# Attention groups 1 and 2 of a hybrid trunk: scores by residue in blocks of 64 by 64, three transposes a half, both groups' values stacked

## The chip, the cores and the metric

The kernel runs on one core of one Trainium2 chip. Its time is the device time of one execution in microseconds (us); the median of the runs is quoted, and the trace is of one profiled execution. In the profile PE is the matrix engine TensorE (PEld its weight loads), DVE is VectorE, ACT ScalarE, POOL GpSimd, SP the engine that issues most DMAs.

## What is computed

Two residual layers on a sequence of 256 tokens of width 1024: a short gated convolution, then a dilated window attention, each followed by a squared-ReLU MLP of width 4096 and a gated per-layer embedding. The change lies in the attention alone. It has three groups of 8 heads of width 128; group g sees keys at distances that are multiples of its dilation, within its window:

```python
DILATED_PATTERNS = ((128, 1), (512, 4), (2048, 16))
...
for g, (window, dilation) in enumerate(DILATED_PATTERNS):
    o_g, lse_g = dilated_window_attention(q[:, :, g], k[:, :, g], v[:, :, g], window, dilation)
    outs.append(o_g)
    lses.append(lse_g)
weights = jax.nn.softmax(jnp.stack(lses, axis=0), axis=0)
o = jnp.sum(weights[..., None] * jnp.stack(outs, axis=0), axis=0)
return o.reshape(b_, s_, hh * dh).astype(h.dtype) @ w_o
```

Weighting the groups by the softmax of their log sums is the same as one softmax over the scores of all three groups side by side, and that is how the kernel does it. With dilation 4, a token meets only tokens of its own residue modulo 4, 64 of the 256; with dilation 16, a part of these.

## The kernel before

A plan, a list of matmul blocks and of steps (`do`), is written out by `make_plan` and walked once; each block names a weight tile, an accumulator and an operand. Weights come from HBM in slabs of up to 8 tiles of 128x128 on SP's queue, and each slab is split into two fp32r halves, `whi` on ScalarE (line 357) and `wlo` on VectorE (line 296), up to five slabs ahead of use. All projections are line 393, in `block`. PSUM is one pool of 8 banks, given out in turn.

In the attention layer the tokens lie in the order of `residue_order`: first by residue modulo 4, so that tokens of one residue are 64 neighbours, and a half of 128 tokens holds two residues. Head after head the plan runs the projections of q and k for groups 0, 1 and 2 (`acc_qk`) and of v (`acc_v`), and between them, one head behind, the steps `scores`, `turn` and `values` of the head before.

- `scores` (lines 674 to 693), for each half b of 128 queries: group 0 as three fp32r matmuls against all 256 keys (L680), then groups 1 and 2 each as one fp32 matmul of the half's 128 queries against the half's 128 keys (L683). The scores fill a bank of 512 columns: 256 of group 0, 128 of group 1, 128 of group 2. One VectorE instruction (L686) scales, adds the mask and takes the maximum; ScalarE takes the exponential with its sum (L690) and scales by the reciprocal (L692). The mask sets to -1e30 what a group does not see, so half of each 128x128 block of groups 1 and 2, where the residues differ, is masked.
- `turn` (lines 695 to 707) transposes the 128x512 probabilities of each half in four pieces (L701), splits those of group 0 in two, and copies those of groups 1 and 2 out of PSUM on ScalarE (L706).
- `values` (lines 709 to 734): group 0 as six fp32r matmuls (L716), then for each half and each of groups 1 and 2 one fp32 matmul (L722), all into one accumulator; ScalarE and VectorE split the result into `y` (L733, L734).
- `v_out` (lines 662 to 671) scales the v projection out of PSUM: group 0 in two halves (L668, L669), groups 1 and 2 as one ScalarE copy of 128x256 for each half of the tokens (L670).

A scheduler orders the instructions of each engine; PE's order follows the plan closely.

Of the kernel before, what the change touches and what calls it, by code (L numbers as in the profile page):

```python
# [9 lines left out]
F32 = mybir.dt.float32  # L10
F32R = mybir.dt.float32r
I32 = mybir.dt.int32
AF = mybir.ActivationFunctionType
ALU = mybir.AluOpType

P = 128
S = 256
# [5 lines left out]
GROUPS = 3  # L23
# [3 lines left out]
NEG = -1e30  # L27
# [13 lines left out]
def residue_order(t):  # L41

    return (t % 4) * 64 + (t % 16 // 4) * 16 + t // 16
# [211 lines left out]
def tile_trunk(ctx: ExitStack, tc: tile.TileContext, plan, slabs, ap, out):  # L255
    nc = tc.nc
# [3 lines left out]
    apool = ctx.enter_context(tc.tile_pool(name="act", bufs=ACT_BUFS))  # L260
# [6 lines left out]
    def act(name, dtype=F32):  # L267
        return apool.tile([P, 2, S], dtype, tag="act", name=name)
# [4 lines left out]
    def pair(name, tag="pair", dtype=F32R):  # L273

        if tag == "pair":
            t = apool.tile([P, 2, 2, S], dtype, tag=tag, bufs=PAIR_BUFS, name=name)
        else:
            t = cpool.tile([P, 2, 2, S], dtype, tag=tag, bufs=1, name=name)
        return t[:, :, 0, :], t[:, :, 1, :], t

    def bank(name):
        return psum.tile([P, 2, S], F32, tag="ps", name=name)
# [6 lines left out]
    def f32(t):  # L289
        return t.bitcast(F32)  # L290

    def flat(t):
        return t.rearrange("p i s -> p (i s)")
# [20 lines left out]
    rstd, rows, cur, mask, by_token = {}, {}, {}, {}, {}  # L314
# [5 lines left out]
    offsets, n = [], 0  # L320
# [6 lines left out]
    for si, s in enumerate(slabs):  # L327
# [3 lines left out]
        at = 0  # L331
# [71 lines left out]
    def close(name):  # L403
        opened.discard(name)

        return acc.pop(name)
# [21 lines left out]
    def split_into(kind, j, src):  # L428
        hi, lo, t = pair(f"{kind}{j}", "pp" if kind in ("p0", "p1") else "pair")
        nc.scalar.activation(hi, src, AF.Copy)  # L430
        sub(lo, src, hi)
        state[kind][j] = (hi, lo, t)
# [146 lines left out]

    def masks_load():  # L580
        for b in (0, 1):
            mask[b] = apool.tile([P, 512], F32, tag="act", name=f"mask{b}")
            nc.sync.dma_start(mask[b], ap["mask"][:, b, :])

    def conv(c):
# [75 lines left out]

    def v_out(head):

        v0, v12 = act(f"v0_{head}", F32R), act(f"v12_{head}")
        for b in (0, 1):
            p, r = flat(close(("v", b, head))), rstd[3][:, b : b + 1]
            hi, lo = v0[:, b, :P], v0[:, b, P:]
            nc.scalar.activation(hi, p[:, :P], AF.Copy, scale=r)  # L668
            nc.vector.scalar_tensor_tensor(lo, p[:, :P], r, f32(hi), ALU.mult, ALU.subtract)  # L669
            nc.scalar.activation(v12[:, b, :], p[:, P : GROUPS * P], AF.Copy, scale=r)  # L670
        cur["v", head] = v0, v12


    def scores(head):
        for b in (0, 1):
            own = slice(b * P, (b + 1) * P)
            ps = psum.tile([P, 512], F32, tag="ps", name=f"sc{head}_{b}")
            hi, lo, _ = state["qk"][head]
            for n, (q, k) in enumerate(((hi, hi), (hi, lo), (lo, hi))):
                nc.tensor.matmul(ps[:, :S], q[:, 0, own], k[:, 1, :], start=n == 0, stop=n == 2)  # L680
            for g in (1, 2):
                t = cur["qk", head, g]
                nc.tensor.matmul(ps[:, (g + 1) * P : (g + 2) * P], t[:, 0, own], t[:, 1, own], start=True, stop=True)  # L683
            sm = flat(act(f"sm{head}_{b}"))
            stats = [spool.tile([P, 1], F32, tag=f"st{n}_{b}", name=f"st{n}_{head}_{b}") for n in range(3)]
            nc.vector.tensor_tensor_reduce(  # L686
                out=sm, in0=ps, in1=mask[b], op0=ALU.add, op1=ALU.max, scale=SCALE, scalar=NEG, accum_out=stats[0]
            )
            nc.vector.tensor_scalar(stats[1], stats[0], -1.0, None, ALU.mult)
            nc.scalar.activation(sm, sm, AF.Exp, bias=stats[1], accum_out=stats[2])  # L690
            nc.vector.reciprocal(stats[2], stats[2])
            nc.scalar.activation(sm, sm, AF.Copy, scale=stats[2])  # L692
            cur["pr", head, b] = sm

    def turn(head):

        ps = [bank(f"tp{head}_{n}") for n in (0, 1)]
        for b in (0, 1):
            sm = cur.pop(("pr", head, b))
            for n in range(4):  # L700
                nc.tensor.transpose(  # L701
                    ps[n // 2][:, n % 2, b * P : (b + 1) * P], sm[:, n * P : (n + 1) * P], ident
                )
        split_into("pT", head, ps[0])
        t = act(f"pT12_{head}")
        nc.scalar.activation(t, ps[1], AF.Copy)  # L706
        cur["pT12", head] = t

    def values(head):
        ps = bank(f"o{head}")  # L710
        v0, v12 = cur.pop(("v", head))
        hi, lo, _ = state["pT"].pop(head)
        for kb in (0, 1):
            vhi, vlo = v0[:, kb, :P], v0[:, kb, P:]
            for n, (a, b) in enumerate(((vhi, hi), (vhi, lo), (vlo, hi))):
                nc.tensor.matmul(  # L716
                    ps[:, 0, :], a, b[:, kb, :], start=kb == 0 and n == 0, stop=False, skip_group_check=True
                )
        t = cur.pop(("pT12", head))
        for b in (0, 1):  # L720
            for g in (0, 1):
                nc.tensor.matmul(  # L722
                    ps[:, 0, b * P : (b + 1) * P],
                    v12[:, b, g * P : (g + 1) * P],
                    t[:, g, b * P : (b + 1) * P],
                    start=False,
                    stop=g == 1,
                    skip_group_check=True,
                )
        if head % 2 == 0:  # L730
            state["y"][head // 2] = pair(f"y{head // 2}")
        hi, lo = (t[:, head % 2, :] for t in state["y"][head // 2][:2])
        nc.scalar.activation(hi, ps[:, 0, :], AF.Copy)  # L733
        nc.vector.tensor_tensor(lo, ps[:, 0, :], f32(hi), ALU.subtract)  # L734
# [76 lines left out]
    def last_scale(b, c):  # L811
# [12 lines left out]
    steps = dict(  # L824
        begin=begin, p_in=p_in, x_in=x_in, add_up=add_up, squares=squares, proj_out=proj_out, stat=stat, stat_rows=stat_rows, conv=conv, mix_out=mix_out, up_out=up_out,
        down_out=down_out, gate_out=gate_out, rope=rope, masks=masks_load, qk_out=qk_out, qk_split=qk_split, v_out=v_out,
        scores=scores, turn=turn, spread=spread, values=values,
        last_load=last_load, turn_h=turn_h, last_gate=last_gate, last_out=last_out, last_rms=last_rms, last_scale=last_scale,
    )
# [21 lines left out]
def masks():  # L851

    import numpy as np

    t = np.argsort([residue_order(t) for t in range(S)])
    m = np.full((P, 2, 512), NEG, np.float32)
    for b in range(2):
        q = t[b * P : (b + 1) * P, None]
        for keys, to, window, step in (
            (t, slice(0, S), 128, 1),  # L860
            (t[b * P : (b + 1) * P], slice(S, S + P), 512, 4),
            (t[b * P : (b + 1) * P], slice(S + P, S + 2 * P), 2048, 16),
        ):
            d = q - keys[None]
            m[:, b, to][(d >= 0) & (d <= window) & (d % step == 0)] = 0.0
    return m


# [56 lines left out]
```

## Time and profile before

| | |
|---|---|
| runs, median | 780.3 us (780.16 to 780.39, 3 runs) |
| profiled execution, its own time | 780.49 us |
| its span, first to last instruction | 778.6 us |
| busy: PE / PEld | 770.2 us / 700.2 us |
| busy: DVE / ACT / POOL | 572.8 us / 442.7 us / 166.8 us |
| HBM read | 139.10 MB, 180 GB/s over the span |

Busy time is the sum in which an engine had an instruction under way. Matmul records overlap: the next one starts before the record of the last ends, so PE's busy time does not say what one matmul costs. The chain of waits does: it follows the work back from the last instruction and gives each piece the time until the next. "mean ns of one" in the groups is the length of a record, and "idle before" the idle time of the engine just before it.

### The profile page before, as it was taken

To read this page: it belongs to the slowest core of one execution; us is meant where nothing else is said; L and a number is where in the kernel's file an instruction comes from. 1 tells how busy PE (TensorE), PEld (TensorE's weight loads), DVE (VectorE), ACT (ScalarE), POOL (GpSimd) and SP (SyncE) were. 2 spreads that over 40 slices of the span, in tenths; PEclk is the share of its full clock that TensorE was granted. 3 is DMA by queue.
4 is the path that set the end of the run, shared out by engine and by line. 5 is a ranking of instruction groups with operands and counts; after the bars stand their busy time and mean duration, and the time that the engine had idled before them with its cause. 6 is when DMAs were issued, how large, how long until landed. Compare 5 with 4: busy or idle time off the path is not lost.

```text
span 778.6 us, 12434 instructions
## 1 busy us (share of the span) xinstructions
PE 770.2 (99%) x4812; PEld 700.2 (90%) x4812; DVE 572.8 (74%) x823; ACT 442.7 (57%) x685; POOL 166.8 (21%) x110
## 2 busy tenths in 40 slices
PE   9999999999999999999999999999999999999996
PEld 9998998888888899989989989989988888888885
DVE  6898779898556669788768768767698887655564
ACT  8655565565444447557655655655675555444453
POOL 0000000000000000177867867865000000000002
PEclk9999999999999999999999999999999999999999
DMA  9865555656555654654455455455465555555521
GB/s 315 301 193 187 189 190 186 192 175 205 184 191 185 192 179 152 204 186 154 149 175 163 151 174 163 153 172 191 134 200 184 189 189 191 188 190 189 188 92 54
DMA packets 42538, 140.95 MB, mean 181 GB/s; under 512 B 4848, under 2 KB 6128, under 8 KB 42480
## 3 DMA queue, kind: packets, MB, share of 16 engines
q1 hardware_dynamic: 41904, 139.52, 55.2%
q8 instruction: 37, 0.61, 0.3%
q10 hardware_dynamic: 576, 0.66, 0.3%
q14 instruction: 21, 0.17, 0.1%
HBM read 139.10 MB, written 1.05 MB: 180 GB/s over the span
## 4 chain that ended last, share of the span: by engine, by line
PE 98%; issue 1%; DVE 0%; POOL 0%; POOLq 0%; DVEq 0%
PE acc_u L393 23%; PE acc_d L393 23%; PE acc_qk L393 17%; PE acc_v L393 9%; PE acc_o L393 6%; PE acc_g L393 5%; PE acc_B L393 3%; PE acc_C L393 3%; PE acc_X L393 3%; PE acc_p L393 1%; PE o L722 1%; PE sc L683 1%; PE tp L701 1%; PE sc L680 1%; PE o L716 1%
## 5 line engine op out<-in xcount | busy, mean ns | idle before, releaser
L296 DVE TENSOR_TENSOR wlo<-raw,whi 128x1024 fp32r<-128x1024 f32 (+2 forms) x277 | 350.6, 1272 | 159.7 <-ACT whi L357 157.4
L357 ACT ACTIVATE whi<-raw 128x1024 fp32r<-128x1024 f32 (+2 forms) x277 | 278.5, 1007 | 214.7 <-PE acc_d L393 77.1
L393 PE MATMUL acc_u<-x,whi 128*128 128x512 f32 x512 | 160.8, 395 | 0.0
L393 PE MATMUL acc_d<-u,whi 128*128 128x512 f32 x512 | 160.8, 395 | 0.0
L393 PE MATMUL acc_qk<-x,whi 128*128 128x512 f32 (+1 forms) x432 | 134.5, 368 | 0.0
L393 PEld LDWEIGHTS acc_d<-u,wlo 128*128 128x128 f32 x512 | 96.2, 188 | 22.7
L393 PEld LDWEIGHTS acc_u<-x,wlo 128*128 128x128 f32 x512 | 96.2, 188 | 22.6
L463 POOL TENSOR_TENSOR n<-v,power 128x2 f32<-128x2 f32 (+1 forms) x6 | 3.9, 651 | 518.2 <-DVE v L488 513.5
L393 PE MATMUL acc_qk<-x,wlo 128*128 128x256 f32 x384 | 107.8, 281 | 0.0
L393 PE MATMUL acc_u<-x,wlo 128*128 128x256 f32 x512 | 101.3, 278 | 0.0
L393 PE MATMUL acc_d<-u,wlo 128*128 128x256 f32 x512 | 100.9, 278 | 0.0
L393 PEld LDWEIGHTS acc_qk<-x,whi 128*128 128x128 f32 x432 | 77.9, 188 | 13.7
L650 POOL TENSOR_TENSOR rot<-qk,sinr 16x512 f32<-16x512 f32 x44 | 78.3, 1781 | 3.0
L393 PEld LDWEIGHTS acc_u<-x,whi 128*128 128x128 f32 x512 | 78.0, 189 | 0.0
L393 PEld LDWEIGHTS acc_d<-u,whi 128*128 128x128 f32 x512 | 77.9, 189 | 0.0
L393 PEld LDWEIGHTS acc_qk<-x,wlo 128*128 128x128 f32 x384 | 72.5, 189 | 0.0
L393 PE MATMUL acc_v<-whi,x 128*128 128x384 f32 x256 | 68.9, 340 | 0.0
L647 POOL TENSOR_TENSOR qk<-qk,cosr 128x512 f32<-128x512 f32 x22 | 36.8, 1671 | 53.7 <-DVE qk L413 41.8
L393 PEld LDWEIGHTS acc_v<-whi,x 128*128 128x128 f32 x256 | 46.6, 188 | 0.0
L393 PE MATMUL acc_o<-y,whi 128*128 128x256 f32 x256 | 46.4, 283 | 0.0
L656 POOL TENSOR_TENSOR qk<-qk,rot 48x512 f32<-48x512 f32 x22 | 42.9, 1950 | 1.7
L393 PE MATMUL acc_v<-wlo,x 128*128 128x384 f32 x128 | 42.9, 335 | 0.0
(175 smaller groups left out, 1028.9 us busy)
## 6 DMA issues: line engine op xcount, KB each, us to landing
raw<-in_w SPq DMA_DIRECT2D x230, 512.0 KB, 3.4
raw<-in_w SPq DMA_DIRECT2D x32, 384.0 KB, 3.1
raw<-in_w SPq DMA_DIRECT2D x10, 256.0 KB, 5.1
h<-in_xT SPq DMA_DIRECT2D x4, 256.0 KB, 5.6
mask<-in_mask SPq DMA_DIRECT2D x2, 256.0 KB, 4.4
gain<-in_gain SPq DMA_DIRECT2D x2, 256.0 KB, 5.9
out<-htg SPq DMA_DIRECT2D x2, 256.0 KB, 2.1
raw<-in_w ACTq DMA_DIRECT2D x2, 128.0 KB, 3.5
```

Source lines behind the costliest of these rows:

```text
L296: nc.vector.tensor_tensor(out, a, f32(b), ALU.subtract)
L357: nc.scalar.activation(hi[:, :width], t[:, :width], AF.Copy)
L393: nc.tensor.matmul(to, a, b, start=n == 0 and name not in opened, stop=n == len(products) - 1 and left[name, half if kind == "n" else 0] == 0,
L463: nc.gpsimd.tensor_tensor(y, v, power[:, : v.shape[1]], ALU.pow)
L647: engine.tensor_tensor(t, p, both(cosr), ALU.mult)
L650: engine.tensor_tensor(r[dst : dst + 16], p[src : src + 16], sinr[src : src + 16].unsqueeze(1).to_broadcast([16, 2, S]), ALU.mult,)
L656: engine.tensor_tensor(t[:48], t[:48], r[:48], ALU.add)
L680: nc.tensor.matmul(ps[:, :S], q[:, 0, own], k[:, 1, :], start=n == 0, stop=n == 2)
L683: nc.tensor.matmul(ps[:, (g + 1) * P : (g + 2) * P], t[:, 0, own], t[:, 1, own], start=True, stop=True)
L701: nc.tensor.transpose(ps[n // 2][:, n % 2, b * P : (b + 1) * P], sm[:, n * P : (n + 1) * P], ident)
L716: nc.tensor.matmul(ps[:, 0, :], a, b[:, kb, :], start=kb == 0 and n == 0, stop=False, skip_group_check=True)
L722: nc.tensor.matmul(ps[:, 0, b * P : (b + 1) * P], v12[:, b, g * P : (g + 1) * P], t[:, g, b * P : (b + 1) * P], start=False, stop=g == 1, ...
```

## The change

The two residues of a half are kept apart in groups 1 and 2. `scores` computes, for each residue r of a half, a 64x64 block of group 1 and one of group 2. The 64 rows of residue 0 get group 1 in columns 256 to 319 and group 2 in 320 to 383; the rows of residue 1 the other way round. The bank then holds 384 columns, and the mask, the softmax and the transposes follow: three pieces of 128 for each half. After the third transpose, column q of residue r has 64 keys of group 1 and 64 of group 2 in its 128 rows. `v_out` lays the values out to match: for residue r, rows of the same residue hold group 1 and the other 64 rows group 2, so it copies blocks of 64 partitions by 128 columns, half of them to other partitions than they came from. `values` then takes for each of the four residues one matmul that sums over both groups at once. The mask tensor shrinks from 512 to 384 columns.

```diff
--- before.py
+++ after.py
@@ -579,7 +579,7 @@
 
     def masks_load():
         for b in (0, 1):
-            mask[b] = apool.tile([P, 512], F32, tag="act", name=f"mask{b}")
+            mask[b] = apool.tile([P, S + P], F32, tag="act", name=f"mask{b}")
             nc.sync.dma_start(mask[b], ap["mask"][:, b, :])
 
     def conv(c):
@@ -661,14 +661,21 @@
 
     def v_out(head):
 
         v0, v12 = act(f"v0_{head}", F32R), act(f"v12_{head}")
         for b in (0, 1):
-            p, r = flat(close(("v", b, head))), rstd[3][:, b : b + 1]
+            p, scale = flat(close(("v", b, head))), rstd[3][:, b : b + 1]
             hi, lo = v0[:, b, :P], v0[:, b, P:]
-            nc.scalar.activation(hi, p[:, :P], AF.Copy, scale=r)
-            nc.vector.scalar_tensor_tensor(lo, p[:, :P], r, f32(hi), ALU.mult, ALU.subtract)
-            nc.scalar.activation(v12[:, b, :], p[:, P : GROUPS * P], AF.Copy, scale=r)
+            nc.scalar.activation(hi, p[:, :P], AF.Copy, scale=scale)
+            nc.vector.scalar_tensor_tensor(lo, p[:, :P], scale, f32(hi), ALU.mult, ALU.subtract)
+            for r in (0, 1):
+                own, other = (slice(n * 64, (n + 1) * 64) for n in (r, 1 - r))
+                for g, to in ((1, own), (2, other)):
+                    nc.scalar.activation(
+                        v12[to, b, r * P : (r + 1) * P], p[own, g * P : (g + 1) * P], AF.Copy, scale=scale[own]
+                    )
         cur["v", head] = v0, v12
 
 
     def scores(head):
@@ -678,10 +685,13 @@
             hi, lo, _ = state["qk"][head]
             for n, (q, k) in enumerate(((hi, hi), (hi, lo), (lo, hi))):
                 nc.tensor.matmul(ps[:, :S], q[:, 0, own], k[:, 1, :], start=n == 0, stop=n == 2)
-            for g in (1, 2):
-                t = cur["qk", head, g]
-                nc.tensor.matmul(ps[:, (g + 1) * P : (g + 2) * P], t[:, 0, own], t[:, 1, own], start=True, stop=True)
-            sm = flat(act(f"sm{head}_{b}"))
+
+            for r in (0, 1):
+                of = slice(b * P + r * 64, b * P + (r + 1) * 64)
+                for g in (1, 2):
+                    t, at = cur["qk", head, g], S + (g - 1 ^ r) * 64
+                    nc.tensor.matmul(ps[r * 64 : (r + 1) * 64, at : at + 64], t[:, 0, of], t[:, 1, of], start=True, stop=True)
+            ps, sm = ps[:, : S + P], flat(act(f"sm{head}_{b}"))[:, : S + P]
             stats = [spool.tile([P, 1], F32, tag=f"st{n}_{b}", name=f"st{n}_{head}_{b}") for n in range(3)]
             nc.vector.tensor_tensor_reduce(
                 out=sm, in0=ps, in1=mask[b], op0=ALU.add, op1=ALU.max, scale=SCALE, scalar=NEG, accum_out=stats[0]
@@ -697,14 +707,13 @@
         ps = [bank(f"tp{head}_{n}") for n in (0, 1)]
         for b in (0, 1):
             sm = cur.pop(("pr", head, b))
-            for n in range(4):
+            for n in range(3):
                 nc.tensor.transpose(
                     ps[n // 2][:, n % 2, b * P : (b + 1) * P], sm[:, n * P : (n + 1) * P], ident
                 )
         split_into("pT", head, ps[0])
-        t = act(f"pT12_{head}")
-        nc.scalar.activation(t, ps[1], AF.Copy)
-        cur["pT12", head] = t
+        t = cur["pT12", head] = act(f"pT12_{head}")[:, 0, :]
+        nc.scalar.activation(t, ps[1][:, 0, :], AF.Copy)
 
     def values(head):
         ps = bank(f"o{head}")
@@ -717,16 +726,16 @@
                     ps[:, 0, :], a, b[:, kb, :], start=kb == 0 and n == 0, stop=False, skip_group_check=True
                 )
         t = cur.pop(("pT12", head))
-        for b in (0, 1):
-            for g in (0, 1):
-                nc.tensor.matmul(
-                    ps[:, 0, b * P : (b + 1) * P],
-                    v12[:, b, g * P : (g + 1) * P],
-                    t[:, g, b * P : (b + 1) * P],
-                    start=False,
-                    stop=g == 1,
-                    skip_group_check=True,
-                )
+        for n in range(4):
+            q, r = slice(n * 64, (n + 1) * 64), n % 2
+            nc.tensor.matmul(
+                ps[:, 0, q],
+                v12[:, n // 2, r * P : (r + 1) * P],
+                t[:, q],
+                start=False,
+                stop=n == 3,
+                skip_group_check=True,
+            )
         if head % 2 == 0:
             state["y"][head // 2] = pair(f"y{head // 2}")
         hi, lo = (t[:, head % 2, :] for t in state["y"][head // 2][:2])
@@ -853,16 +862,18 @@
     import numpy as np
 
     t = np.argsort([residue_order(t) for t in range(S)])
-    m = np.full((P, 2, 512), NEG, np.float32)
+    m = np.full((P, 2, S + P), NEG, np.float32)
     for b in range(2):
         q = t[b * P : (b + 1) * P, None]
-        for keys, to, window, step in (
-            (t, slice(0, S), 128, 1),
-            (t[b * P : (b + 1) * P], slice(S, S + P), 512, 4),
-            (t[b * P : (b + 1) * P], slice(S + P, S + 2 * P), 2048, 16),
-        ):
-            d = q - keys[None]
-            m[:, b, to][(d >= 0) & (d <= window) & (d % step == 0)] = 0.0
+        for r, rows in enumerate((slice(0, 64), slice(64, P))):
+            own = t[b * P : (b + 1) * P][rows]
+            for keys, at, window, step in (
+                (t, 0, 128, 1),
+                (own, S + r * 64, 512, 4),
+                (own, S + (1 - r) * 64, 2048, 16),
+            ):
+                d = q[rows] - keys[None]
+                m[rows, b, at : at + len(keys)][(d >= 0) & (d <= window) & (d % step == 0)] = 0.0
     return m
```

On PE, the scores of head 2 (`sc2_0` and `sc2_1` are the banks of the two halves, `qk_2_1` and `qk_2_2` q and k of groups 1 and 2). Before:

```order
L680 MATMUL sc2_0_4327<-qk2_4206 128x256 x3
L683 MATMUL sc2_0_4327<-qk_2_1_4095 128x128
L683 MATMUL sc2_0_4327<-qk_2_2_4165 128x128
L680 MATMUL sc2_1_4342<-qk2_4206 128x256 x3
L683 MATMUL sc2_1_4342<-qk_2_1_4095 128x128
L683 MATMUL sc2_1_4342<-qk_2_2_4165 128x128
L393 MATMUL acc_qk_3_1_0_4357<-x3_0_3154,wlo147_4197 128x256
```

With the change:

```order
L687 MATMUL sc2_0_4349<-qk2_4222 128x256 x3
L693 MATMUL sc2_0_4349<-qk_2_1_4113 64x64
L693 MATMUL sc2_0_4349<-qk_2_2_4181 64x64
L693 MATMUL sc2_0_4349<-qk_2_1_4113 64x64
L693 MATMUL sc2_0_4349<-qk_2_2_4181 64x64
L687 MATMUL sc2_1_4366<-qk2_4222 128x256 x3
L693 MATMUL sc2_1_4366<-qk_2_1_4113 64x64
L693 MATMUL sc2_1_4366<-qk_2_2_4181 64x64
L693 MATMUL sc2_1_4366<-qk_2_1_4113 64x64
L693 MATMUL sc2_1_4366<-qk_2_2_4181 64x64
L393 MATMUL acc_qk_3_1_0_4383<-x3_0_3154,wlo147_4213 128x256
```

The three matmuls of group 0 stay; behind them stand four of 64x64 instead of two of 128x128, in each half, and the projection of head 3 follows as before.

On ScalarE, `v_out` of head 2 and what follows it to the softmax of the same head (`whi` are weight splits). Before:

```order
L668 ACTIVATE v0_2_4264<-acc_v_1_2_4184,n2_3_3506 128x128
L357 ACTIVATE whi150_4275<-raw150_4175 128x1024
L670 ACTIVATE v12_2_4265<-acc_v_0_2_4174,n2_3_3506 128x256
L670 ACTIVATE v12_2_4265<-acc_v_1_2_4184,n2_3_3506 128x256
L357 ACTIVATE whi151_4298<-raw151_4194 128x768
L412 ACTIVATE qk_3_0_4318<-acc_qk_3_0_0_4272 128x256
L412 ACTIVATE qk_3_0_4318<-acc_qk_3_0_1_4281 128x256
L357 ACTIVATE whi152_4360<-raw152_4215 128x768
L690 ACTIVATE sm2_0_4333,st2_2_0_4336<-sm2_0_4333,st1_2_0_4335 128x512
L690 ACTIVATE sm2_1_4348,st2_2_1_4351<-sm2_1_4348,st1_2_1_4350 128x512
L692 ACTIVATE sm2_0_4333<-sm2_0_4333,st2_2_0_4336 128x512
L692 ACTIVATE sm2_1_4348<-sm2_1_4348,st2_2_1_4351 128x512
```

With the change:

```order
L669 ACTIVATE v0_2_4280<-acc_v_1_2_4200,n2_3_3506 128x128
L357 ACTIVATE whi150_4297<-raw150_4191 128x1024
L674 ACTIVATE v12_2_4281<-acc_v_0_2_4190,n2_3_3506 64x128 x4
L674 ACTIVATE v12_2_4281<-acc_v_1_2_4200,n2_3_3506 64x128 x4
L357 ACTIVATE whi151_4320<-raw151_4210 128x768
L412 ACTIVATE qk_3_0_4340<-acc_qk_3_0_0_4294 128x256
L412 ACTIVATE qk_3_0_4340<-acc_qk_3_0_1_4303 128x256
L357 ACTIVATE whi152_4386<-raw152_4231 128x768
L700 ACTIVATE sm2_0_4357,st2_2_0_4360<-sm2_0_4357,st1_2_0_4359 128x384
L702 ACTIVATE sm2_0_4357<-sm2_0_4357,st2_2_0_4360 128x384
L700 ACTIVATE sm2_1_4374,st2_2_1_4377<-sm2_1_4374,st1_2_1_4376 128x384
L357 ACTIVATE whi153_4409<-raw153_4262 128x768
```

Each `x4` is four copies where there was one; the softmax passes have 384 columns, and the scaling of the first half now stands ahead of the second half's exponential.

## Rows read from the trace of the kernel before

**Rows 1.** The cores view, whole span

```profile
core 0: 778.6 us, clock 0.998
```

**Rows 2.** The page: busy us (share) xcount, the chain's shares by engine and line

```profile
PE 770.2 (99%) x4812; PEld 700.2 (90%) x4812; DVE 572.8 (74%) x823; ACT 442.7 (57%) x685; POOL 166.8 (21%) x110
...
PE 98%; issue 1%; DVE 0%; POOL 0%; POOLq 0%; DVEq 0%
PE acc_u L393 23%; PE acc_d L393 23%; PE acc_qk L393 17%; PE acc_v L393 9%; PE acc_o L393 6%; PE acc_g L393 5%; PE acc_B L393 3%; PE acc_C L393 3%; PE acc_X L393 3%; PE acc_p L393 1%; PE o L722 1%; PE sc L683 1%; PE tp L701 1%; PE sc L680 1%; PE o L716 1%
```

**Rows 3.** The waits, engine PE: engine, line, releaser, us, times, longest

```profile
PE warm L523 <- DVE power L519: 1.0, 1, 1.0
```

**Rows 4.** The chain in order of time, 395 to 425 us: start, us, what

```profile
395.92 0.35 PE sc L680 x3
396.27 0.44 PE sc L683 x4
396.71 0.36 PE sc L680 x3
397.07 0.44 PE sc L683 x4
397.52 11.11 PE acc_qk L393 x64
408.63 0.87 PE tp L701 x8
409.50 6.27 PE acc_v L393 x36
415.77 0.71 PE o L716 x6
416.48 0.89 PE o L722 x8
```

**Rows 5.** Groups by line and form: busy us, mean ns, idle before

```profile
L683 PE MATMUL sc<-qk 128*128 128x128 f32 x64 | 9.7, 274 | 0.0
...
L683 PEld LDWEIGHTS sc<-qk 128*128 128x128 f32 x64 | 8.5, 191 | 0.0
L722 PE MATMUL o<-pT,v 128*128 128x128 f32 x64 | 8.4, 274 | 0.0
L701 PE MATMUL tp<-ident,sm 128*128 128x128 f32 x64 | 8.3, 272 | 0.0
...
L478 PE MATMUL ssq<-ones,tot 128*128 128x2 f32 x16 | 2.0, 230 | 0.0
```

**Rows 6.** The timeline of PEld, 29.6 to 31 us: start, us, what

```profile
29.69 0.54 PEld L478 LDWEIGHTS ssq<-ones,tot 128*128 128x128 f32 x4
30.14 0.19 PEld L393 LDWEIGHTS acc_C<-x,wlo 128*128 128x128 f32 x1
```

**Rows 7.** Line L478 alone: ns min/median/max, first and last start

```profile
L478 PE MATMUL ssq<-ones,tot x16: 165/251/251, 29.8 to 753.6; 128*128 128x2 f32 x16
```

**Rows 8.** Groups by line and form, ScalarE copies and scalings

```profile
L670 ACT ACTIVATE v<-acc_v,n 128x256 f32<-128x256 f32 x16 | 6.7, 471 | 3.5 <-DVE v L669 3.5
...
L668 ACT ACTIVATE v<-acc_v,n 128x128 fp32r<-128x128 f32 x16 | 5.8, 368 | 8.6 <-PE acc_v L393 8.6
...
L706 ACT ACTIVATE pT<-tp 128x512 f32<-128x512 f32 x8 | 4.7, 589 | 0.0
...
L733 ACT ACTIVATE y<-o 128x256 fp32r<-128x256 f32 x8 | 3.1, 384 | 4.6 <-PE o L722 4.6
```

**Rows 9.** Busy time in stretches, 395 to 420 us: PE, PEld, DVE, ACT, POOL

```profile
395.00:420.00 25.00, 25.00 (x158) 23.42 (x158) 18.80 (x27) 14.99 (x27) 20.73 (x12) 1.00 0.51 162
```

**Rows 10.** The timeline of ACT and then the chain, 419 to 446 us

```profile
420.71 0.83 ACT L670 ACTIVATE v<-acc_v,n 128x256 f32<-128x256 f32 x2
422.32 0.84 ACT L357 ACTIVATE whi<-raw 128x768 fp32r<-128x768 f32 x1 [0.78 <-ACT v L670]
...
426.61 11.11 PE acc_qk L393 x64
```

## The prediction

> **What bounds the kernel now.** First the cores view: one core, span 778.6 us, granted clock 0.998, so the whole span is at the upper of TensorE's two levels, 2.4 GHz, but for a sliver [rows 1]. Then the page's busy times and chain: PE is busy in 99% of the span, and 98% of the chain that ended last is PE, nearly all of it the projections of line 393 [rows 2]. Then who makes PE wait: once, for 1.0 us, at the very start [rows 3]. So time is what PE's instructions take, laid end to end; the other engines count only if they become late enough to stop PE. The change touches PE in three steps, `scores`, `turn` and `values`, whose lines (L680, L683, L701, L716, L722) hold about 1% of the chain each. The chain in order of time through one head gives their true price, which busy times do not, since matmul records overlap: three fp32r score matmuls 0.35 us, four L683 passes 0.44, eight transposes 0.87, six L716 0.71, eight L722 0.89 [rows 4]. The count of passes needs care: 2 halves x 2 groups x 8 heads are 32 matmuls of L683, but the trace has 64, and 64 of L722 for 32 [rows 5]. A plain fp32 matmul runs as two passes, each with its own weight load; the transposes, 64 for 64, are one pass.
>
> **What sets the price of a small pass.** L683, L701 and L722 all move 128 columns and all take 0.109 to 0.111 us [rows 4]. The one smaller form of the kernel is the sum of squares, L478, which moves 2 columns over a 128-column stationary block [rows 5]. Its four loads start at 29.69 and the next line's at 30.14 [rows 6]: 0.113 us a pass. 2 moving columns cost the same as 128. So a pass of this size is not bound by what moves, but by its stationary block, or by a fixed price. Long matmuls argue against a fixed price added to each: 64 matmuls of acc_qk, half of 512 and half of 256 columns, take 11.11 us, 0.452 ns a column; 36 of acc_v with 384 columns take 6.27 us, 0.454 ns [rows 4]. That is proportional, with nothing left over. A floor below which no pass can go is not excluded.
>
> **The change, part by part.**
>
> *Turn.* Three transposes a half instead of four: 2 x 8 heads = 16 passes fewer at 0.87/8 = 0.109 us: **-1.74 us**. These lie directly on the chain.
>
> *Values.* Per head four fp32 matmuls of 128 moving columns become four of 64; still 128-column stationary blocks, still 64 passes in all. If the price followed moving columns it would fall by 64 x 0.0555 = 3.6 us. The 2-column row says it does not [rows 6]: **0**, with -3.6 as an end I hardly believe. Stacking two groups into one contraction halves the arithmetic but not the number of stationary blocks: before 4 per head, after 4.
>
> *Scores.* 4 matmuls per head become 8, of 64 stationary by 64 moving columns: 64 passes at 0.110 = 7.04 us become 128 passes. No row has a stationary block under 128 columns. If price follows the block, a pass is 0.055 and the sum is again 7.04; if 0.110 is a floor, it is 14.08. I take the half, because of the proportionality above: **0**, other end +7.04. The Trainium skill (TensorE: Matmul & The Clock Gate, LDWEIGHTS) gives a load as the block's columns divided by 1.2, in ns; worked out from that, as estimates, 107 ns for 128 columns and 53 for 64, and the sum would be the same. The trace agrees for 128 columns (0.110 us a pass); no run here shows 64.
>
> *Going in and out of the half-wide shape.* In each half of each head the 64-wide passes stand between 128-wide ones: 2 changes in and out x 2 halves x 8 heads = 32. Today a load runs behind the matmul before it, which is why a record of 0.19 us load and 0.27 us matmul costs only 0.11 [rows 5]. If the array must be empty before its columns are used another way, that cover is lost at each change. Lower end: 0 per change; today's alternation between fp32r (L680) and fp32 (L683) costs nothing beyond the passes [rows 4]. Upper end: load and matmul records in full, 0.191 + 0.274 - 0.110 = 0.355. In between, the 2-column matmul: its record of 0.251 [rows 7], nearly all of it way through the array, less its spacing of 0.113 leaves a tail of 0.14 that today lies under the next pass. I take that, since an emptying array loses just this tail while the next load can run beside it: 32 x 0.14 = **+4.5 us**; ends 0 and +11.4.
>
> The Trainium skill (TensorEngine Tiling (Array Packing), Key Properties) speaks against the change here: a change of tiling mode, not merely of tile, drains the engine. It gives no price; no run here shows it yet. By its drain the sum is the forecast's, without it the first rival's.
>
> *ScalarE.* `v_out` swaps 2 copies of 128x256 (0.471) for 8 of 64 partitions x 128; nearest row 128x128 from PSUM, 0.368 [rows 8]: +2.0 us a head. Against it, four softmax passes lose 128 columns at (0.589-0.384)/256 = 0.8 ns a column, 0.1 us each, and the pT12 copy falls from 0.589 to 0.384 [rows 8]: -0.6. Net +1.4 us a head. Cover: in 25 us of a head's stage ScalarE is busy for 15.0 [rows 9]. What waits behind it: the release of acc_v's two banks, done at 421.5 in this head, then about 423.5, while the next projection group opens at 426.6 [rows 10]; and the weight split `whi` queued behind v_out, which has slabs in hand. Price 0; if the 10 us of idle were gone, 8 x 1.4 = 11 us.
>
> *The rest.* The reduction over scores on VectorE and the two mask loads shrink by a quarter. Neither holds PE: 0.
>
> **Sum.** -1.74 + 0 + 0 + 4.5 = +2.7 us on the profiled execution's 780.49: 783.2. The median of the runs, 780.3, lies 0.19 lower, so **783.0 us**, slower by 0.35%. About 0.2%, 1.6 us, is what a measurement of this kernel can tell from no change.
>
> **Rivals.**
> 1. *The change of shape is free* (other side). Then only the transposes count: -1.74, 778.6 us. It decides wherever a change costs under 1.74/32 = 0.054 us. For it: today's two kinds of matmul alternate without loss [rows 4]. Against: they use the same 128 columns, and nothing in the trace changes width. The Trainium skill (same page and section) also says tiles work independently; should the first pass of the second 64 rows run beside the last of the first, once a half, that is 16 x 0.055 = 0.9 us more, 777.7.
> 2. *0.110 is a floor per pass.* Scores then cost +7.04: with free changes +5.3, 785.6; with the tail +9.8, 790.1. For it: no row below 0.109. Against: the proportional long matmuls.
> 3. *Everything is exposed at a change*, more than 0.2 us each: from +4.7 (785.0) to +9.6 (789.9).
> 4. *Values do follow the moving columns*, -3.6: with the tail -0.8 (779.5), without -5.3 (775.0). The 2-column row speaks against it.
>
> **How the numbers follow.** Forecast (a change costs 0.05 to 0.2, so -0.1 to +4.7: 780.2 to 785.0) 0.45; rival 1 0.22; rival 2 0.12; rival 3 0.16; rival 4 0.05. Faster by over 0.2% needs nearly all of rival 1's gain, half its chance, and most of rival 4: 0.15. Within 0.2%: the other half of rival 1, the rest of rival 4 and the forecast's part below 0.1 us a change: 0.25. Slower: 0.60. The range 778.4 to 788.5 leaves out rival 1's overlap and rival 4 below, the upper half of rivals 2 and 3 above, about 2 in 10.
>
> **What would show it.** In the chain, a head's turn falls from 0.87 to 0.65 and the L722 group stays at 0.89. The four 64x64 matmuls of a half, 8 passes, should take 0.44 plus some 0.28 for the two changes: 0.7 us; 0.44 means rival 1, 0.88 or more evenly spaced means rival 2; gaps in PEld at the first and last of the eight mean rival 3. L722 at half price is rival 4. A wait of PE other than at the start, or ScalarE on the chain, would make the whole reading wrong.

## The result and the profile after

| | before | with the change |
|---|---|---|
| median of 12 runs | 780.49 us (780.16 to 780.94) | 782.39 us (781.81 to 782.75) |
| ratio, 95% interval | | 1.0023 (1.0015 to 1.0031) |
| span of the profiled execution | 778.6 us | 780.8 us |

The change costs 1.9 us, 0.23% (1.2 to 2.4 us by the interval). Forecast were +2.7 us and 783.0. The direction and the size were right; two terms that the forecast did not have, a gain and a loss, lie under that sum and partly cancel.

The cores view, and then who makes PE wait, with the change:

```profile
core 0: 780.8 us, clock 0.999
```

```profile
PE tp L711 <- ACT sm L702: 1.2, 1, 1.2
PE warm L523 <- DVE power L519: 1.0, 1, 1.0
```

The clock is as in [rows 1], so nothing is due to it. In [rows 3] the start was PE's only wait; now there is a second one of 1.2 us, at a transpose.

The chain in order of time with the change, for the head of [rows 4] (start, us, what; L687 is L680 of before, L693 L683, L711 L701, L725 L716, L731 L722):

```profile
398.09 0.35 PE sc L687 x3
398.44 0.39 PE sc L693 x8
398.82 0.55 PE sc L687 x3
399.37 0.39 PE sc L693 x8
399.76 11.30 PE acc_qk L393 x64
411.06 0.66 PE tp L711 x6
411.71 6.24 PE acc_v L393 x36
417.96 0.71 PE o L725 x6
418.67 0.84 PE o L731 x8
419.51 2.14 PE acc_v L393 x12
```

Piece by piece against [rows 4]: the transposes take 0.66 us for 0.87, -0.21 a head. The stacked values take 0.84 for 0.89, but the piece behind them 2.14 where it took 2.08: nothing. The scores take 0.35 + 0.39 + 0.55 + 0.39 = 1.68, and 0.19 more lies in the projection behind them (11.30 for 11.11): 1.87 for 0.35 + 0.44 + 0.36 + 0.44 = 1.59, +0.28 a head. Times 8: -1.7, 0 and +2.2 us. The wait comes on top, in head 0, PE's timeline:

```profile
356.95 0.34 PE L393 MATMUL acc_v<-whi,x 128*128 128x384 f32 x1
358.46 1.05 PE L711 MATMUL tp<-ident,sm 128*128 128x128 f32 x6 [1.17 <-ACT sm L702]
359.27 0.42 PE L393 MATMUL acc_v<-whi,x 128*128 128x384 f32 x1
```

The first transpose starts 1.51 us after the matmul before it, where 0.18 is usual: 1.3 us late. The transposes behind it are spread out too, those of the second half waiting once more: from the first transpose to the next projection head 0 takes 0.81 us, the other heads 0.57. In all the wait costs 1.6 us, and the sum is +2.1, where 1.9 was measured. The heads are not quite alike: the projection behind the scores of head 1 takes 11.50 us, 0.2 more than behind the others, in e1, e2, e3 and e6 too, and no run says why.

Groups by line and form of the new passes (busy us, mean ns of one, idle before):

```profile
L693 PE MATMUL sc<-qk 128*64 128x64 f32 x128 | 7.3, 234 | 0.0
...
L693 PEld LDWEIGHTS sc<-qk 128*64 128x64 f32 x128 | 5.1, 136 | 2.1
```

128 passes, as counted, now with 64 stationary columns (`128*64`); loads have records of 136 ns where 128 columns had 191 [rows 5].

**How the wait comes about.** Head 0's v_out, ScalarE's timeline, before:

```profile
337.69 0.84 ACT L670 ACTIVATE v<-acc_v,n 128x256 f32<-128x256 f32 x2 [1.83 <-DVE v L669]
338.42 0.39 ACT L412 ACTIVATE qk<-acc_qk 128x256 f32<-128x256 f32 x1
```

and with the change:

```profile
337.97 2.99 ACT L674 ACTIVATE v<-acc_v,n 64x128 f32<-64x128 f32 x8 [1.80 <-DVE v L670]
340.99 0.66 ACT L412 ACTIVATE qk<-acc_qk 128x256 f32<-128x256 f32 x2
```

The eight copies take 2.99 us for 0.84, +2.15 (forecast +2.0 by the nearest row). What was not seen is what stands right behind them on ScalarE here: L412, the sums of head 1, now 2.6 us late. VectorE waits for these. Its timeline before:

```profile
341.11 1.81 DVE L296 TENSOR_TENSOR wlo<-raw,whi 128x768 fp32r<-128x768 f32 x2
...
344.49 1.77 DVE L296 TENSOR_TENSOR wlo<-raw,whi 128x768 fp32r<-128x768 f32 x1 [0.30 <-ACT whi L357]
347.26 1.24 DVE L296 TENSOR_TENSOR wlo<-raw,whi 128x1024 fp32r<-128x1024 f32 x1 [0.99 <-ACT whi L357]
...
351.36 0.68 DVE L686 CUSTOM_DVE_ANT_0 sm<-sc,mask 128x512 f32<-128x512 f32 x1
```

and with the change:

```profile
341.40 0.76 DVE L413 TENSOR_TENSOR qk<-acc_qk,qk 128x256 f32<-128x256 f32 x2 [1.21 <-ACT qk L412]
...
344.00 4.00 DVE L296 TENSOR_TENSOR wlo<-raw,whi 128x768 fp32r<-128x768 f32 x2
...
348.59 4.84 DVE L296 TENSOR_TENSOR wlo<-raw,whi 128x768 fp32r<-128x768 f32 x2
...
355.06 0.54 DVE L696 CUSTOM_DVE_ANT_0 sm<-sc,mask 128x384 f32<-128x384 f32 x1
```

Two weight splits that took 1.81 us take 4.00. The next line, 4.84 us, merges a split of 128x768 and one of 128x1024, 2.62 and 2.30 us where they took 1.77 and 1.24. The reduction over the scores of head 0 comes 3.7 us later, at 355.1. GpSimd runs its rotary embedding beside the splits all the while. The transpose of head 0 is due about 357 and gets its probabilities at 358.4. The Trainium skill (GPSIMD Engine Reference, Specifications) has GpSimd share its interfaces to SBUF with VectorE, with contention where VectorE reads two operands from there, as these splits do; the slow splits agree, but no run here separates the two engines. Nor is it shown which of them gives way: before the change GpSimd ran beside the first pair of splits too, and there its own instruction was the slow one (L647, 3.42 us, where the next takes 1.28).

### The profile page after: what moved, and what is told of

It is laid out like the page before. It is cut to its first block, busy times and chain, and to the rows that moved or that the text cites. A ratio compares the mean times of both kernels' runs of the same rounds, so it can differ in the third digit from the quotient of the medians.

```text
span 780.8 us, 12591 instructions
## 1 busy us (share of the span) xinstructions
PE 771.3 (99%) x4860; PEld 697.4 (89%) x4860; DVE 584.2 (75%) x823; ACT 454.0 (58%) x733; POOL 165.9 (21%) x110
## 4 chain that ended last, share of the span: by engine, by line
PE 94%; DVE 3%; issue 2%; ACT 1%; POOL 0%; POOLq 0%; DVEq 0%
PE acc_u L393 23%; PE acc_d L393 23%; PE acc_qk L393 15%; PE acc_v L393 7%; PE acc_o L393 6%; PE acc_g L393 5%; PE acc_B L393 3%; PE acc_C L393 3%; PE acc_X L393 3%; PE acc_p L393 1%; DVE wlo L296 1%; PE o L731 1%; PE sc L687 1%; PE o L725 1%; PE tp L711 1%
## 5 line engine op out<-in xcount | busy, mean ns | idle before, releaser
L296 DVE TENSOR_TENSOR wlo<-raw,whi 128x1024 fp32r<-128x1024 f32 (+2 forms) x277 | 364.3, 1323 | 152.7 <-ACT whi L357 150.3
L650 POOL TENSOR_TENSOR rot<-qk,sinr 16x512 f32<-16x512 f32 x44 | 82.3, 1870 | 3.0
L647 POOL TENSOR_TENSOR qk<-qk,cosr 128x512 f32<-128x512 f32 x22 | 31.5, 1431 | 57.9 <-DVE qk L413 41.1
```

What stands on the lines that cost most here:

```text
L296: nc.vector.tensor_tensor(out, a, f32(b), ALU.subtract)
L647: engine.tensor_tensor(t, p, both(cosr), ALU.mult)
L650: engine.tensor_tensor(r[dst : dst + 16], p[src : src + 16], sinr[src : src + 16].unsqueeze(1).to_broadcast([16, 2, S]), ALU.mult,)
```

## The experiments

Theory A, from this trace: a change into or out of the 64-wide shape costs about 0.17 us of PE; the passes of the two residues run side by side; the wait comes from v_out of head 0. Rivals: the cost is in the passes (B), the pairs that run together are another kind (C), the wait comes from VectorE and GpSimd alone.

**e1, scores grouped.** Group 0 of both halves first, then all 64x64 matmuls:

```diff
-        for b in (0, 1):
-            ... group 0 of half b; 64x64 blocks of half b
+        for b in (0, 1):
+            ... group 0 of half b
+        for b in (0, 1):
+            ... 64x64 blocks of half b
```

> The changed kernel with its score matmuls in another order: in each head the six 128-wide matmuls of group 0, of both halves, first, then all eight 64x64 matmuls. PE goes into the 64-wide shape and out of it once a head instead of twice: 16 changes instead of 32, the same matmuls. Theory A (each change of shape costs about 0.17 us of PE time, as the trace of the changed kernel has it: 0.09 more than a usual step on the way in, about 0.15 on the way out, shared): 16 x 0.17 = 2.7 us less than the changed kernel's 782.4, so 779.7. Rival B (the cost sits in the 64-wide passes themselves, not in the changes): same as the changed kernel, 782.4.

Measured: 780.20 us, 0.9995 (0.9987 to 1.0004) of before. Its chain:

```profile
397.45 0.70 PE sc L687 x6
398.16 0.66 PE sc L693 x16
398.82 11.30 PE acc_qk L393 x64
```

2.2 us less than the change, in the same passes. By the chain the head's scores take 0.70 + 0.66 + 0.19 = 1.55 for 1.87: two changes fewer are 0.32 us, 0.16 each as the mean of in and out, times 16 is 2.6. The wait of head 0 grew to 1.5 us and took 0.3 of that back. B is out: the same passes cost less when they stand together.

**e2, v_out of head 0 later.** The step stands behind the first sums of head 1:

```diff
-    plan += ... + v(0, range(2, NK)) + [("do", "v_out", 0)]
+    plan += ... + v(0, range(2, NK))
...
-        plan += [("do", "qk_split", 0)] if late else steps[0]
+        plan += [("do", "qk_split", 0), ("do", "v_out", 0)] if late else steps[0]
```

> The changed kernel with v_out of head 0 moved behind the first sums and the split of head 1 (its copies are needed only much later). Theory A (PE's 1.2 us wait for the softmax of head 0 in the changed kernel comes from the eight copies of v_out, which hold up ScalarE's sums for head 1 by about 2 us, and with them VectorE's weight splits, which then run beside GpSimd and take twice as long): the wait goes, 1.3 us less than 782.4, so 781.1. Rival B (VectorE is late there whatever v_out does, because it and GpSimd collide): wait stays, 782.4.

Measured: 780.87 us, 1.0002 (0.9993 to 1.0011). 1.5 us less than the change. PE's waits, and VectorE's reduction with the splits ahead of it:

```profile
PE warm L523 <- DVE power L519: 1.0, 1, 1.0
PE acc_p L393 <- ACT whi L357: 0.3, 1, 0.3
```

```profile
346.09 3.61 DVE L296 TENSOR_TENSOR wlo<-raw,whi 128x768 fp32r<-128x768 f32 x2
...
351.31 0.55 DVE L696 CUSTOM_DVE_ANT_0 sm<-sc,mask 128x384 f32<-128x384 f32 x1
```

The wait at the transpose is gone and the reduction is back at 351.3. The pair of splits ahead of it still takes 3.61 us, 3.01 before the change, and that does not stop PE: the rival, that VectorE is late whatever v_out does, is out. That the copies in front of the sums bring the wait is shown by this; how much of the 3.7 us is their own 2.15 and how much the slower splits behind them is not. A new wait of 0.3 us, for a weight split, costs a little back.

**e3, both edits.**

> Both of the last two edits together. Theory A: the gains add, 2.7 + 1.3 = 4.0 us less than 782.4, so 778.4, which would be 2.1 us faster than the kernel before. Rival B on both: 782.4. If only the order of the scores counts: 779.7.

Measured: 778.52 us, 0.9973 (0.9962 to 0.9984). As expected, and faster than before: the wait is gone, the pairs of passes pay for the 16 changes that are left (scores of a head 1.55 us, 1.59 before), and the transposes' gain shows. PE waits only at the start.

**e4, residues kept apart.** A matmul of group 0 between the blocks of one residue and of the other. It stands inside the accumulation of group 0 in its bank, so this run's output is changed; the matmuls are all there.

```diff
-            ... three matmuls of group 0; residue 0's two 64x64; residue 1's two
+            ... group 0 first; residue 0's two 64x64; group 0 second; residue 1's two; group 0 third
```

> The changed kernel with the 64x64 matmuls of the two residues of a half kept apart by a matmul of group 0: 64 changes of shape instead of 32, the same matmuls. Theory A (0.17 us a change, and the passes of the two residues, which write different halves of the rows, run side by side, eight in 0.24 us where one residue's four alone take 4 x 0.058 = 0.23): 32 x 0.17 = 5.4 for the changes and 16 x 0.22 = 3.5 for passes that no longer overlap, 791.3. Rival C (the two passes of one fp32 matmul overlap, not those of two residues): 5.4 alone, 787.8. Rival B (changes are free): at most 785.9.

Measured: 789.93 us, 1.012 (1.0104 to 1.0135). The chain of a head, and the loads of one residue's block in the PEld timeline:

```profile
398.67 0.11 PE sc L687
398.78 0.38 PE sc L692 x4
399.15 0.31 PE sc L687
399.47 0.38 PE sc L692 x4
399.84 0.43 PE sc L687 x2
400.28 0.38 PE sc L692 x4
400.65 0.31 PE sc L687
400.97 0.38 PE sc L692 x4
401.34 0.32 PE sc L687
401.66 11.10 PE acc_qk L393 x64
```

```profile
399.40 0.31 PEld L692 LDWEIGHTS sc<-qk 128*64 128x64 f32 x4
```

The changed kernel, same view:

```profile
398.36 0.32 PEld L693 LDWEIGHTS sc<-qk 128*64 128x64 f32 x8
```

Four passes of one residue take 0.31 us where eight of two residues take 0.32. That is what separates A from C: passes for different halves of the PSUM rows run side by side, passes for the same half go one after another, (0.31 - 0.136)/3 = 0.058 us apart. The time is 1.4 us under the 791.3 expected, and the wait accounts for it: the expectation had kept it in its base of 782.4, and here, with PE itself later, the first transpose of head 0 is 0.2 us late instead of 1.3. Less these 1.1 us, 790.2 would have stood there.

Three numbers per head give the prices: scores less 0.70 for group 0 are 1.17 us with 4 changes, 0.85 with 2 (e1), 2.29 with 8 and no pairs (e4). The first two give 0.16 us a change and 0.53 for the 16 passes in pairs, 0.066 a pair; e4 then leaves 2.29 - 1.28 = 1.01 for 16 passes alone, 0.063 each. The other way round, with the 0.058 us that the loads show, e4 alone gives (2.29 - 0.93)/8 = 0.17 us a change.

**e5 and e6, the values 64 wide too.** If pairs are that cheap, the values can use them: each 128-column block is cut in two for the two halves of the output rows. In e6 in the old place, in e5 beside the scores of the next head, so that both share one way in and out. On top of e3:

```diff
-            nc.tensor.matmul(ps[:, 0, q], v12[:, n // 2, r * P : (r + 1) * P], t[:, q], ...
+            for d in (0, 1):
+                nc.tensor.matmul(
+                    ps[d * 64 : (d + 1) * 64, 0, q],
+                    v12[:, n // 2, r * P + d * 64 : r * P + (d + 1) * 64], t[:, q], ...
```

> The version with both edits (scores grouped, v_out of head 0 later), and in it the stacked values of a head in stationary blocks of 64 columns too, two for each 128, one for each half of the output rows; and for heads 0 to 6 the values stand right beside the scores of the next head, so that both share one way in and one way out. Theory A (64-wide passes cost 0.058 us for a pair on the two halves of the rows, a change about 0.16): 16 passes of values in 8 pairs take 0.46 us a head where 8 passes of 128 columns take 0.87: 7 heads x 0.41 = 2.9 us less, head 7 with its own two changes about 0.1 less: 3.0 less than 778.5, so 775.5. Rival D (passes that add to a bank already written by 128-wide matmuls don't pair up, 0.058 each): 16 x 0.058 = 0.93, no gain, 778.5 to 779.0.

> The same 64-column blocks for the values, but in the old place, so that each head goes in and out of the 64-wide shape once more: 16 more changes. Theory A: 8 x (-0.41 + 2 x 0.16) = -0.7 us against the version with both edits, 777.8. Rival D (no pairs): 8 x (+0.06 + 0.32) = +3.0, 781.5.

Measured: e5 775.25 us, 0.9933 (0.9921 to 0.9946); e6 777.89 us, 0.9967 (0.9955 to 0.9979). Both within 0.3 us of theory A; D is out. The chain of e5:

```profile
421.63 0.71 PE o L732 x6
422.34 0.71 PE sc L690 x6
423.05 0.62 PE o L741 x16
423.67 0.51 PE sc L698 x16
```

With one change behind and one ahead, 16 narrow passes of values and 16 of scores take 0.62 + 0.51 and 0.19 in the next piece, 1.32 us. Values and scores of groups 1 and 2 took 0.89 + 0.88 = 1.77 before [rows 4]. e5 is the best version found, 5.2 us faster than before.

## Why the prediction was right

- *Turn*, -1.74: measured 8 x 0.21 = -1.7. Right, and wholly on the chain.
- *Values*, 0: right. The 2-column row [rows 6] told it: over 128 stationary columns a pass costs 0.11 us with 2, 64 or 128 moving ones, and a pass of the scores, with 64 moving columns too but 64 stationary ones, 0.063. Rival 4 is out.
- *Scores, passes*, 0: wrong by 2.8 us, to the good. Half the block for half the price was right for a pass that runs alone (0.063, forecast 0.055). The step that failed is to lay all 128 end to end. The two residues write different rows and run in pairs: 16 x 0.033 x 8 = 4.2 us, not 7.04. Rival 1 named this, after the Trainium skill (TensorEngine Tiling (Array Packing), Key Properties), but only for one pass at a seam; e4 shows that it holds for all of them, although the code issues both groups of one residue before the other. Rival 2, a floor of 0.11, is out. With its two changes a half's four blocks take (1.87 - 0.70)/2 = 0.59 us, where 0.7 was to be seen.
- *Changes of shape*, 32 x 0.14 = +4.5: measured 32 x 0.16 = +5.1 (e1, e4). A fixed price at each change was right, and the tail of the 2-column matmul [rows 7] came near it; that the price is this tail is argued, since no run separates it from another fixed loss. The prices of rivals 1 (under 0.054) and 3 (over 0.2) are out. The Trainium skill's drain on a change of tiling mode (TensorEngine Tiling (Array Packing), Key Properties) agrees with a price at each change.
- *ScalarE*, 0: wrong by 1.6 us. The load was right (the copies of all heads take 23.2 us for 6.7, +2.1 us a head; forecast +2.0) and there was idle time enough over the head [rows 9]. The step that failed is to look at a late head [rows 10] and take it for all: in head 0 the sums of the next head, which VectorE needs, stand straight behind v_out. The prediction said that a wait of PE elsewhere would make its whole reading wrong; it was one stall, not the bound.

Together -1.7 + 0 - 2.8 + 5.1 + 1.6 = +2.2 (the pieces of the chain gave 2.1), where 1.9 was measured (1.2 to 2.4). The two missed terms, -2.8 and +1.6, are each about as large as the result, so its nearness to the forecast is partly luck; that the change of shape decides was not.

## What to carry to other kernels

Price a small matmul that loads new weights each time by its stationary block, not by what moves (here up to 128 moving columns): find the row with the fewest moving columns first. Narrow stationary blocks pay if both halves of the rows are in use at the same time, and if many of them stand together, since each way in and out of the narrow shape costs a fixed time; group them before judging them. Cover by idle time must be checked at the first and tightest round of a loop, by what stands next in the queue, not by the share of busy time in a middle one.

## What the runs showed of the hardware that was not expected

Two streams of 64-column passes, for rows 0 to 63 and for rows 64 to 127, ran side by side although the program issues four passes of the first before the first of the second: eight passes in 0.32 us where four alone take 0.31. They pair as well when they add to a bank that 128-wide matmuls have written (e5, e6). The slow weight splits, up to 2.6 us for 128x768 where 0.94 to 1.77 were seen before the change, were not expected in that size.
